# A hybrid decoder trunk: the strided pairs of the mixer wait for another mark, and the second sum of h is issued in more steps

## The chip, the cores and the metric

The kernel runs on one core of a Trainium2 chip. The time is that of one execution on the device in microseconds. Before the change it has a median of 2717.23 us over three runs (2716.2 to 2718.05). The profiled execution took 2714.47 us, with a span of 2712.6 us in its trace.

The engines are named as in the profile: PE is TensorE (matrix products), PEld its weight loads, DVE is VectorE, ACT is ScalarE, POOL is GpSimd, and SP is the queue that issues DMA transfers.

## The reference

Two layers (`DEPTH = 2`) work on 1024 tokens of width 1024, in float32:

```
for l in range(DEPTH):
    h = rmsnorm(x, norm1[l])
    proj = h @ w_in[l]                 # q, k, v of mixer A, q, k, v of mixer B, two gates
    o_a = dilated_mixture(qa, ka, va)  # 3 groups of 4 heads: (window, dilation) (128,1) (512,4) (2048,16)
    o_b = stick_breaking_attention(qb, kb, vb)           # 4 heads
    g_a, g_b = sigmoid(gate_pre + b_gate[l]) split in two
    x = x + (g_a * (o_a @ w_br[l, :OUT_A]) + g_b * (o_b @ w_br[l, OUT_A:])) @ w_o[l]
    h2 = rmsnorm(x, norm2[l])
    x = x + (gelu(causal_conv(h2 @ w_up[l], gate half)) * value half) @ w_down[l]
return rmsnorm(x, norm_f)
```

What matters here is the first half of a layer, the mixer: the product `h @ w_in[l]` and the attention of mixers A and B.

## The kernel before

**Products in two parts.** Each float32 operand is split into a high part and a rest (`split`, lines 129 and 130: a cast on ACT, a subtraction on DVE), and three matmuls make one product (high by high, high by rest, rest by high).

**Plain products and strided pairs.** In the mixer, `h` is held in two halves of the tokens, each in eight blocks of 128 features (`hh`, `hl` in the trace). Keys, queries and values of the first dilated group and of mixer B are plain products. All the other columns of `w_in` (group 1 and 2 of mixer A, which are read with a stride over the tokens, and the gates) are computed in pairs of column blocks by a scheme that makes seven products of half size do for eight. One of the seven is computed as a plain product (`ahead` in `pair`, `r_ps` in the trace, 14 units). The other six, in five accumulations, are the unit `run` in `pair_rest` (`i_a`, `i_c` in the trace): four pairs of keys and queries (`kqs`), two of values (`vs`) and eight of gates (`gates`). Each pair begins with seven opening stages: it loads its weights (`in_a`), POOL and the splits make combinations of their blocks, and the kept plain product is loaded into `u`.

**The sums of h.** The pairs also need sums of h's blocks, S[1] to S[4]. `block_sums` plans them as a list of small entries: S[3] after the marks B14 and B17, S[1] after N01s, S[2] after N11s, S[4] after the plain units. The same tile (`h_sum`) is worked on from one sum to the next: `first` makes S[1] on POOL, `further` turns it into the next sum with two DVE operations per block (lines 921 and 922), and `in_two` splits each block (`t_hi`, `t_lo`; S[4] is written into `hh`, `hl` of the first half). `series(after, t, f, lag, gap)` puts the sum of block i at step `i * gap` and its split `lag` steps later; each step is an entry of the list, an empty one too.

**What sets the order.** The order on PE is written out by hand: PE's instructions run as the program issues them. ACT, DVE, POOL and SP have a planner, which takes what is ready by priority. The priority follows the place in the program; the splits of attention's parts (`p0h`, `p0l`) and the folds are raised by 200 places.

`attend` goes through the attention items: B00 to B17 (mixer B), N00, N01, N10, N11 (the first dilated group, two pairs of heads), T00 to T17 (the other two groups). An item has scores, turns (transposes of a block of probabilities, line 701 for N) and applies (products with v, line 713 for N); a turn's result is split (`p0h` on ACT, `p0l` on DVE) before the apply reads it. The scores of the next item stand between the turns and applies of the one before where they can. `late`, the last apply of an item, is put behind the first turn of the next item. An item's mark with an "s" (N11s) is set when its last score has been issued.

After each score, turn and apply `attend` calls `dense.advance(rate)`. It first calls `aside`, which takes one entry from the list of sums if its marks are there, then adds the rate (0.85 for the N items) and, for each whole number, makes one `step` of the dense stream: two blocks of a product, six matmuls. A unit of the dense stream is chosen by `choose`: the first of `main` if its marks are there (a strided pair only when the plain list is empty), else a plain unit, else a gate pair, but those only after a first strided pair has started. The next unit is chosen and made ready ahead of its turn, one opening stage a step. If nothing can be chosen, `step` does nothing and `advance` sets the sum of rates to zero. When the first strided pair starts, all that is left of the list of sums is issued at once.

T00 can't begin before its keys are fetched, which is set by a count of dense steps after the pairs of both values and of the first keys and queries are done (`fetch`, `at`); until then `until` calls `aside` and `step` in turn, with no attention between.

Of the kernel before, what the change touches and what calls it, by code (L numbers as in the profile page):

```python
# [47 lines left out]
def f32(ap):  # L48
    return ap.bitcast(F32)
# [3 lines left out]
def trunk_kernel(ctx, tc, x, norm1, w_in, b_gate, w_br, w_o, norm2, w_up, conv_w, conv_b, w_down, norm_f, out, depth=None, probe=None):  # L53
# [71 lines left out]
    def quarter(name, dtype=F32, c=HF):  # L125
        return sb.tile([P, 2048 // c, c], dtype, tag="xa", bufs=4, name=name)

    def split(hi, lo, src):
        act.copy(hi, src)  # L129
        dve.tensor_tensor(lo, src, f32(hi), ALU.subtract)  # L130
# [315 lines left out]
    def new_s(t):  # L446
        hi, lo = big("t_hi", F32R), big("t_lo", F32R)
        S[t] = [tuple(x.rearrange("p a (b c) -> p (a b) c", c=HF)[:, i, :] for x in (hi, lo)) for i in range(4)]
# [428 lines left out]
    def half(n, k):  # L877
        return [(H[n][0][:, 4 * k + i, :], H[n][1][:, 4 * k + i, :]) for i in range(4)]
# [13 lines left out]
            if i == 1:  # L892
                yield

    def block_sums():


        keep = {}
        S.clear()

        def at(t, i):
            if t == 3 and i < 2:
                if "o" not in keep:
                    keep["o"] = sb.tile([P, 2, HF], F32, tag="ot", name="h_sum2")
                return keep["o"][:, i, :]
            if "r" not in keep:
                keep["r"] = quarter("h_sum")
            return keep["r"][:, i, :]

        def first(t, a, b, i):  # L910
            r, (ah, al), (bh, bl) = at(t, i), a()[i], b()[i]
            pool.tensor_tensor(r, f32(al), f32(bl), ALU.subtract)
            pool.tensor_tensor(r, r, f32(ah), ALU.add)
            pool.tensor_tensor(r, r, f32(bh), ALU.subtract)

        def further(t, a, i):
            if t == 4:

                S[4] = half(0, 0)
            r, (ah, al) = keep["r"][:, i, :], a()[i]  # L920
            dve.tensor_tensor(r, f32(ah), r, ALU.subtract)
            dve.tensor_tensor(r, r, f32(al), ALU.add)

        def in_two(t, i):
            if t not in S:
                new_s(t)
            split(*S[t][i], at(t, i))

        b11, b12, b21, b22 = (lambda n=n, k=k: half(n, k) for k in range(2) for n in (1, 0))
        todo = []  # L930

        def plan(after, steps):

            for k in range(max(steps) + 1):
                todo.append((after, lambda fs=steps.get(k, ()): [g() for g in fs]))

        def series(after, t, f, lag, gap):
            steps = {}
            for i in range(4):
                steps.setdefault(i * gap, []).append(lambda i=i: f(i))  # L940
                steps.setdefault(i * gap + lag, []).append(lambda i=i: in_two(t, i))
            plan(after, steps)

        def third(i):
            return lambda: first(3, b22, b12, i)

        def cast(i):
            return lambda: in_two(3, i)

        plan({"B14"}, {0: [third(0)], 6: [third(1)]})  # L950
        plan({"B17"}, {0: [third(2)], 1: [cast(0)], 4: [cast(1)], 6: [third(3)], 9: [cast(2)], 14: [cast(3)]})
        series({"N01s"}, 1, lambda i: first(1, b12, b11, i), 7, 6)
        series({"N11s"}, 2, lambda i: further(2, b22, i), 1, 1)
        series({"plain", "01", "v0"}, 4, lambda i: further(4, b21, i), 1, 1)
        return todo

# [106 lines left out]
    def pair_kq(dense, l, g, pr):  # L1063
        off = 256 * g + P * pr

        def put(c, n, x, psum):
            hi = small("kq_h", F32R)
            lo = small("kq_l", F32R) if psum else x.bitcast(F32R)
            hv, lv, xv = (t if t is x and psum else t.rearrange("p (r j) -> p r j", r=4) for t in (hi, lo, x))
            if c:  # L1070
                act.mul(hv, xv, -SCALE)
                dve.scalar_tensor_tensor(lv, xv, -SCALE, f32(hv), ALU.mult, ALU.subtract)
            else:
                act.copy(hv, xv)
                dve.tensor_tensor(lv, xv, f32(hv), ALU.subtract)
            for src, kind in ((hv, 2), (lv, 1)) if c else ((hv, 3), (lv, 4)):
                there = tk[pr][:, :, 6 * (g - 1) + kind, n * P : (n + 1) * P]
                nc.sync.dma_start(there.rearrange("r p j -> p r j"), f32(src))
            if (c, n) == (1, 1):
                dense.done.add(f"{g}{pr}")  # L1080

        return pair(dense, l, (OFF_KA + off, OFF_QA + off), True, put)

    def pair_v(dense, l, g):


        def turn(c, n, f):
            tp = bank("s", "v_t")
            for r in range(4):
                pe.transpose(tp[:, r * P : (r + 1) * P], f[:, r * P : (r + 1) * P], ident)  # L1090
            for r in (0, 2):
                tw = tp[:, r * P : (r + 2) * P].rearrange("p (r h c) -> p r h c", r=2, h=2)
                vv = small("vv", F32R).rearrange("p (r h c) -> p r h c", r=2, h=2)
                act.copy(vv[:, :, :, 0:64], tw)
                dve.tensor_tensor(vv[:, :, :, 64:128], tw, f32(vv[:, :, :, 0:64]), ALU.subtract)
                for h in range(2):
                    there = tv[c][h, r : r + 2, :, g - 1, n * P : (n + 1) * P]
                    nc.sync.dma_start(there.rearrange("r p c -> p r c"), f32(vv[:, :, h, :]))
            if (c, n) == (1, 1):
                dense.done.add(f"v{g}")  # L1100

        def put(c, n, x, psum):
            f = x
            if psum:
                f = small("vf")
                act.copy(f.rearrange("p (r j) -> p r j", r=4), x)
            dense.at(4, lambda: turn(c, n, f))

        off = OFF_VA + 256 * g
        return pair(dense, l, (off, off + P), True, put)  # L1110
# [35 lines left out]
    def mixer(l, pending):  # L1146
# [9 lines left out]
        dense = Dense()  # L1156
        vs = {g: pair_v(dense, l, g) for g in (1, 2)}
        kqs = {(g, pr): pair_kq(dense, l, g, pr) for pr in range(2) for g in (1, 2)}
# [2 lines left out]
        dense.seven = [rest() for _, rest, _ in gates]  # L1161
        order = [vs[1], *(kqs[g, 0] for g in (1, 2)), vs[2], *(kqs[g, 1] for g in (1, 2)), *gates]
        dense.loads = [load for _, _, load in order]
        dense.side = [({"B02"}, zeros)] * (l == 0) + block_sums()

        def kq(name, pr, after, off, scale):
            offk, offq = (OFF_KB, OFF_QB) if name == "b" else (OFF_KA, OFF_QA)
            return [
                (None, after, keys(("k" + name, pr), l, offk + off), False),
                (name + str(pr), after, queries(("q" + name, pr), l, offq + off, scale), False),  # L1170
            ]
# [3 lines left out]
            ("v0", set(), values("v0", l, OFF_VA), False),  # L1175
            *kq("0", 0, {"B07s"}, 0, -SCALE),
            *kq("0", 1, {"B17s"}, P, -SCALE),
            (None, {"N11s"}, vs[1][1](), True),
            *((None, {"N11s"}, kqs[g, 0][1](), True) for g in (1, 2)),
            (None, {"N11s"}, vs[2][1](), True),  # L1180
            *((None, {"N11s"}, kqs[g, 1][1](), True) for g in (1, 2)),
        ]
        items = []
        for pr in range(2):
# [30 lines left out]
        todo = [(n, e0 + i) for e0 in range(0, KD, 2) for n in range(2) for i in range(2)]  # L1215
# [632 lines left out]
    with tc.manual_schedule(engines={mybir.EngineType.PE}):  # L1848
        pending = first()
        next(pending)  # L1850
        for l in range(depth):
            pending = mixer(l, pending)
            pending = ffn(l, pending, enter(l + 1) if l + 1 < depth else leave)
# [21 lines left out]
```

## Time and profile before

| | |
|---|---|
| median of three runs | 2717.23 us |
| profiled execution | 2714.47 us |
| its span | 2712.6 us |
| PE busy | 2657.8 us |
| DVE busy | 2105.9 us |
| ACT busy | 1330.4 us |
| POOL busy | 742.1 us |

A row of the profile's timeline gives the start in the span, the duration, the engine, the line of the kernel, what is written from what, the shapes, and how many instructions it merges. In brackets stands the idle time of the engine before the row and what ended it. PE's matmuls overlap, so that the distance from one start to the next says what one takes. A row of the table of stretches gives its bounds, its length, the busy time of PE, PEld, DVE, ACT and POOL with their counts, the granted clock of PE as a share of full speed, the busy share of the DMA engines, and GB/s.

### The profile page before, as it was taken

To read this page: it belongs to the slowest core of one execution; us is meant where nothing else is said; L and a number is where in the kernel's file an instruction comes from. 1 tells how busy PE (TensorE), PEld (TensorE's weight loads), DVE (VectorE), ACT (ScalarE), POOL (GpSimd) and SP (SyncE) were. 2 spreads that over 40 slices of the span, in tenths; PEclk is the share of its full clock that TensorE was granted. 3 is DMA by queue.
4 is the path that set the end of the run, shared out by engine and by line. 5 is a ranking of instruction groups with operands and counts; after the bars stand their busy time and mean duration, and the time that the engine had idled before them with its cause. 6 is when DMAs were issued, how large, how long until landed. Compare 5 with 4: busy or idle time off the path is not lost. (4 is left out here: it accounts for less than half of the span.)

```text
span 2712.6 us, 37003 instructions
## 1 busy us (share of the span) xinstructions
PE 2657.8 (98%) x13098; PEld 2227.5 (82%) x13098; DVE 2105.9 (78%) x3104; ACT 1330.4 (49%) x2458; POOL 742.1 (27%) x537
## 2 busy tenths in 40 slices
PE   8999999999999999999999989999999999999999
PEld 8877788888888888888888778888788888888888
DVE  6877876675789988897658888766858888998865
ACT  5656534464455555432335665434545545554225
POOL 2004133322233434321220041332212433443210
PEclk9999999999999999999999999999999999999999
DMA  4023389863235444688401234997722444446863
GB/s 153 20 80 123 123 229 246 207 226 121 85 117 171 141 154 147 223 320 320 154 32 36 84 111 136 250 230 211 248 85 79 148 152 143 171 141 253 333 246 122
DMA packets 397637, 445.72 MB, mean 164 GB/s; under 512 B 21660, under 2 KB 318988, under 8 KB 395916
## 3 DMA queue, kind: packets, MB, share of 16 engines
q1 hardware_dynamic: 397452, 443.35, 51.4%
q8 instruction: 104, 1.70, 0.3%
q14 instruction: 81, 0.66, 0.1%
HBM read 300.61 MB, written 142.67 MB: 163 GB/s over the span
## 5 line engine op out<-in xcount | busy, mean ns | idle before, releaser
L130 DVE TENSOR_TENSOR w_lo<-up_a,w_hi 128x512 fp32r<-128x512 f32 x240 | 237.2, 995 | 20.5 <-ACT w_hi L129 20.5
L129 ACT CAST w_hi<-up_a 128x512 fp32r<-128x512 f32 x240 | 149.5, 623 | 184.1 <-PE u_a L890 45.6
L1631 DVE TENSOR_TENSOR x<-x,d_ps 128x512 f32<-128x512 f32 (+1 forms) x228 | 152.2, 672 | 76.9 <-PE d_ps L1625 76.0
L1362 POOL TENSOR_TENSOR cv<-cv 128x512 f32<-128x512 f32 x88 | 132.1, 1513 | 248.8 <-DVE cv L1357 138.9
L130 DVE TENSOR_TENSOR w_lo<-w_raw,w_hi 128x512 fp32r<-128x512 f32 x176 | 132.5, 756 | 67.8 <-ACT w_hi L129 67.3
L129 ACT CAST w_hi<-w_raw 128x512 fp32r<-128x512 f32 x176 | 109.2, 621 | 125.9 <-PE o_ps L156 68.6
L129 ACT CAST w_hi<-in_a 128x512 fp32r<-128x512 f32 x140 | 86.8, 620 | 147.6 <-PE i_a L890 83.2
L130 DVE TENSOR_TENSOR g<-cv,g 128x512 fp32r<-128x512 f32 x154 | 152.4, 991 | 5.2 <-ACT g L129 2.7
L1623 PE MATMUL d_ps<-gd_in,w_hi 128*128 128x512 f32 (+1 forms) x340 | 130.2, 383 | 1.3 <-ACT w_hi L129 1.1
L1625 PE MATMUL d_ps<-gd_in,w_lo 128*128 128x512 f32 (+1 forms) x340 | 129.8, 382 | 0.0
L1624 PE MATMUL d_ps<-gd_in,w_hi 128*128 128x512 f32 (+1 forms) x340 | 129.7, 382 | 0.0
L889 PE MATMUL u_a<-hh,w_hi 128*128 128x512 f32 x320 | 124.7, 390 | 0.5 <-DVE u L1513 0.5
L889 PE MATMUL u_a<-t_hi,w_hi 128*128 128x512 f32 x320 | 124.6, 389 | 0.0
L891 PE MATMUL u_a<-t_hi,w_lo 128*128 128x512 f32 x320 | 124.5, 389 | 0.0
L890 PE MATMUL u_a<-hl,w_hi 128*128 128x512 f32 x320 | 124.5, 389 | 0.0
L891 PE MATMUL u_a<-hh,w_lo 128*128 128x512 f32 x320 | 124.5, 389 | 0.0
L890 PE MATMUL u_a<-t_lo,w_hi 128*128 128x512 f32 x320 | 124.5, 389 | 0.0
L130 DVE TENSOR_TENSOR w_lo<-in_a,w_hi 128x512 fp32r<-128x512 f32 x140 | 116.0, 828 | 4.1 <-ACT w_hi L129 3.7
L1018 POOL TENSOR_TENSOR in_a<-in_a 128x512 f32<-128x512 f32 x28 | 38.0, 1357 | 278.9 <-DVE w_lo L130 278.9
L627 DVE TENSOR_TENSOR_SCAN stay<-stay,zero 128x128 f32<-128x128 f32 (+3 forms) x64 | 89.0, 1390 | 32.2 <-ACT stay L625 31.6
L1623 PE MATMUL d_ps<-gd_in,wd 128*128 128x512 f32 (+1 forms) x292 | 113.9, 390 | 0.0
L129 ACT CAST g<-cv 128x512 fp32r<-128x512 f32 x154 | 95.0, 617 | 38.2 <-POOL cv L1362 29.7
(390 smaller groups left out, 8747.7 us busy)
## 6 DMA issues: line engine op xcount, KB each, us to landing
gd<-g SPq DMA_DIRECT2D x154, 512.0 KB, 3.7
gd_in<-gd SPq DMA_DIRECT2D x154, 512.0 KB, 6.4
up_a<-in_w_up_dram SPq DMA_DIRECT2D x80, 512.0 KB, 5.8
in_a<-in_w_in_dram SPq DMA_DIRECT2D x56, 512.0 KB, 6.2
w_raw<-in_w_in_dram SPq DMA_DIRECT2D x104, 256.0 KB, 3.0
t_kq<-tk SPq DMA_DIRECT2D x64, 384.0 KB, 7.8
wd_raw<-in_w_down_dram SPq DMA_DIRECT2D x22, 1024.0 KB, 13.0
gin<-gs SPq DMA_DIRECT2D x32, 512.0 KB, 4.4
```

Source lines behind the costliest of these rows:

```text
L129: act.copy(hi, src)
L130: dve.tensor_tensor(lo, src, f32(hi), ALU.subtract)
L627: dve.tensor_tensor_scan(rev, rev, zero[:, 0:1].to_broadcast([P, L]), 1.0, ALU.mult, ALU.add)
L889: pe.matmul(o, w[0][:, c], rh, start=(first and i == 0), stop=False, skip_group_check=True)
L890: pe.matmul(o, w[0][:, c], rl, start=False, stop=False, skip_group_check=True)
L891: pe.matmul(o, w[1][:, c], rh, start=False, stop=(last and i == 3), skip_group_check=True)
L1018: pool.tensor_tensor(a11, a22, a11, ALU.subtract)
L1362: return lambda: pool.tensor_tensor(dst, a, b, ALU.subtract)
L1623: pe.matmul(o[:, sub], wh[:, c], gh[:, sub], start=(i == 0 and k in (0, 4, 5)), stop=False, skip_group_check=True)
L1624: pe.matmul(o[:, sub], wh[:, c], gl[:, sub], start=False, stop=False, skip_group_check=True)
L1625: pe.matmul(o[:, sub], wl[:, c], gh[:, sub], start=False, stop=(i == m - 1), skip_group_check=True)
L1631: dve.tensor_tensor(x, x, o[:, sub], ALU.add)
```

## The change

The second sum is planned with a gap of 2 steps in place of 1, so that each block's sum and each block's split have an entry of their own. Behind them stands a new entry, which waits for nothing and sets the mark T2. The six strided pairs of keys, queries and values in `main` wait for T2 and no longer for N11s. `block_sums` gets the set of marks for it. What is computed stays the same.

```
-    def block_sums():
+    def block_sums(done):
...
-        series({"N11s"}, 2, lambda i: further(2, b22, i), 1, 1)
+        series({"N11s"}, 2, lambda i: further(2, b22, i), 1, 2)
+        todo.append((set(), lambda: done.add("T2")))
         series({"plain", "01", "v0"}, 4, lambda i: further(4, b21, i), 1, 1)
...
-        dense.side = [({"B02"}, zeros)] * (l == 0) + block_sums()
+        dense.side = [({"B02"}, zeros)] * (l == 0) + block_sums(dense.done)
...
-            (None, {"N11s"}, vs[1][1](), True),
-            *((None, {"N11s"}, kqs[g, 0][1](), True) for g in (1, 2)),
-            (None, {"N11s"}, vs[2][1](), True),
-            *((None, {"N11s"}, kqs[g, 1][1](), True) for g in (1, 2)),
+            (None, {"T2"}, vs[1][1](), True),
+            *((None, {"T2"}, kqs[g, 0][1](), True) for g in (1, 2)),
+            (None, {"T2"}, vs[2][1](), True),
+            *((None, {"T2"}, kqs[g, 1][1](), True) for g in (1, 2)),
```

## The prediction

> **What bounds the kernel now.** First the page's busy times and its chain of waits, then the busy time by stages, then the order of TensorE's instructions, and last the rows of the engines that feed it.
>
> ```profile
> span 2712.6 us, 37003 instructions
> PE 2657.8 (98%) x13098; PEld 2227.5 (82%) x13098; DVE 2105.9 (78%) x3104; ACT 1330.4 (49%) x2458; POOL 742.1 (27%) x537
> ```
>
> TensorE (PE) is busy 98% of the span: whatever leaves it idle is paid in full, and there are 2712.6 - 2657.8 = 55 us of idle time that a better order could win. The change moves a unit of PE's work, so I look at the stages around it, in both layers:
>
> ```profile
> 314.00:326.00 12.00, 12.00 (x64) 10.05 (x64) 12.00 (x20) 7.79 (x18) 6.76 (x4) 1.00 0.52 154
> 326.00:339.00 13.00, 12.08 (x65) 9.90 (x64) 12.63 (x24) 6.62 (x13) 0.33 (x1) 1.00 0.20 69
> 339.00:395.00 56.00, 56.00 (x260) 46.32 (x259) 41.20 (x59) 20.85 (x40) 22.68 (x16) 1.00 0.77 211
> 1671.00:1684.00 13.00, 12.05 (x65) 9.89 (x64) 12.63 (x24) 6.59 (x14) 0.57 (x1) 1.00 0.24 78
> ```
>
> After the stretch's bounds and length stand the busy us of PE, its weight loads, VectorE (DVE), ScalarE (ACT) and GpSimd (POOL). From 339 to 395 us PE has no idle time at all. From 326 to 339 it is idle 0.92 us, and DVE is full: 12.63 of 13. Layer 1 repeats it at 1671. PE's rows there (start, duration; the idle time before it in brackets):
>
> ```profile
> 313.71 0.28 PE L585 MATMUL z<-kt,ql 128*128 128x256 f32 x1
> 313.83 0.40 PE L155 MATMUL r_ps<-hh,w_hi 128*128 128x512 f32 x1
> 315.22 0.60 PE L701 MATMUL t<-ident,p 128*128 128x128 f32 x4
> ...
> 326.03 0.28 PE L713 MATMUL o<-p0h,v 128*128 128x256 f32 x1
> 326.51 0.40 PE L889 MATMUL i_a<-t_hi,w_hi 128*128 128x512 f32 x1
> 327.90 0.49 PE L701 MATMUL t<-ident,p 128*128 128x128 f32 x3
> 328.14 0.47 PE L889 MATMUL i_a<-t_hi,w_hi 128*128 128x512 f32 x1
> 329.62 0.28 PE L713 MATMUL o<-p0h,v 128*128 128x256 f32 x1
> 330.05 0.50 PE L889 MATMUL i_c<-t_hi,w_hi 128*128 128x512 f32 x1
> 331.57 0.60 PE L701 MATMUL t<-ident,p 128*128 128x128 f32 x4
> 331.92 0.31 PE L713 MATMUL o<-p0h,v 128*128 128x128 f32 x1
> 332.92 0.33 PE L713 MATMUL o<-p0l,v 128*128 128x128 f32 x1 [0.69 <-DVE p0l L130]
> 333.37 0.40 PE L889 MATMUL i_c<-t_hi,w_hi 128*128 128x512 f32 x1
> 334.77 0.27 PE L701 MATMUL t<-ident,p 128*128 128x128 f32 x1
> 336.26 0.28 PE L713 MATMUL o<-p0h,v 128*128 128x256 f32 x1
> 338.61 0.22 PE L713 MATMUL o<-p0h,v 128*128 128x128 f32 x1
> 338.81 0.48 PE L889 MATMUL i_c<-hh,w_hi 128*128 128x512 f32 x1
> ```
>
> I call six 512-wide matmuls of the dense stream a chunk: 315.22 - 313.83 = 1.39 us. The last score of item N11 is issued at 313.71, and N11s is set. The item's turns (`t`, L701) and applies (`o`, L713) follow, with chunks between them as cover. The last plain product ends at 326.03, and the first strided pair takes over without a gap at 326.51. Between the apply at 326.03 and the chunk at 338.81 stand six chunks of the pair. With `a` for apply and `t` for turn: a0, c1, t2, c2, a1, c3, t3, a2, c4, t4, c5, a3, c6, a4, and c7 at 338.81.
>
> **The change, part by part.** No arithmetic is added or removed.
>
> *When the mark comes.* The side list gives up one entry at each advance, the call after each score, turn or apply. The plan for B17 has 15 entries (0 to 14) and the first sum's 26 (3 x 6 + 7 = 25, from 0). From B17's mark to N11s the items give 12 + 11 + 4 + 8 = 35 advances: the rest of N00 with three of N01's scores; N01 with N00's last apply and its own; N10's four scores; N10 up to N11's last score. So 41 - 35 = 6 entries of the first sum are left when N11s is set. After it come 16 advances: five in N10 (score, t3, a2, t4, a3) and eleven in N11. Before, the pair is free at once and starts at the ninth, when the plain units have run out, just after a0; this is what the rows show. After the change the second sum takes 8 entries (steps 0 to 7) in place of 5, and the mark one more: 6 + 8 + 1 = 15, so T2 is set at the fifteenth advance, just after a3.
>
> *What PE does meanwhile.* At the ninth advance the plain list is empty, the gates may not start before a strided pair has, and `step` finds nothing: the advances in between run no dense work. One chunk goes at the fifteenth, the next after a4. Five of six chunks leave the tail and are done behind a4, in the stretch where PE is full: 5 x 1.39 = 6.95 us there. Everything from then on keeps its order, since T00's fetch hangs on the count of chunks, not on time.
>
> *What that frees.* From 326.03 to 338.81 are 12.78 us. The six chunks between the rows above take 1.39 + 1.48 + 1.52 + 1.40 + 1.49 + 1.4 = 8.7 (the fifth from the end of t4 at 334.77, the sixth as the others), the attention's own issue some 2.65, and the rest, 1.4, is waiting. After: 2.65 + one chunk of 1.4 + the new waits W, then the five chunks, 6.95. So c7 comes at 326.03 + 4.05 + 6.95 + W = 337.03 + W in place of 338.81: the layer loses W - 1.8 us. Without waits it would win. W is what the trace doesn't show, so it is bounded by the rows that feed the applies:
>
> ```profile
> 325.35 1.79 DVE L130 TENSOR_TENSOR hl<-h_sum,hh 128x512 fp32r<-128x512 f32 x2
> 327.66 0.67 DVE L600 TENSOR_TENSOR on<-o,fold 64x512 f32<-64x512 f32 x1
> 328.86 0.54 DVE L130 TENSOR_TENSOR p0l<-t,p0h 128x384 fp32r<-128x384 f32 x1
> 329.33 0.67 DVE L988 TENSOR_TENSOR rf<-q1s,r_ps 128x512 f32<-128x512 f32 x1
> 332.33 0.54 DVE L130 TENSOR_TENSOR p0l<-t,p0h 128x384 fp32r<-128x384 f32 x1
> 336.02 0.68 DVE L130 TENSOR_TENSOR p0l<-t,p0h 128x512 fp32r<-128x512 f32 x1
> ...
> 327.12 0.48 ACT L129 CAST p0h<-t 128x384 fp32r<-128x384 f32 x1
> 330.63 0.62 ACT L129 CAST hh<-h_sum 128x512 fp32r<-128x512 f32 x1 [2.50 <-DVE h_sum L922]
> 331.15 0.47 ACT L129 CAST p0h<-t 128x384 fp32r<-128x384 f32 x1
> ```
>
> Low end: each apply waits only for its own chain, 0.48 + 0.54 (p0h, p0l) and some 0.1 for three hand-overs. With t3 in between, a2 can start 1.15 us after t2, and so on; then c2 starts near 331.3 and W is about 1.2: the layer wins 0.6 us. High end: DVE keeps its whole order, so that the third and fourth parts come at 336.02 and later as now; then a3 ends at about 337, c1 and a4 at 338.9, W is 8.9 and the layer loses 7.1.
>
> I take a value nearer the low end, by the order of the planner. Up to a0 nothing that PE does has moved, and so the planner's order on DVE stands until p0l of t1 at 328.86: a1 can't start before 329.40, though PE is ready at 326.8. That is 2.6 us. After it, the turns are closer together, so that the five DVE operations which now fill the 3 us between the p0l at 328.86 and that at 332.33 shrink to about one (0.67): a2 waits 0.3. For a3, ACT first folds a1's bank, and DVE has that fold (0.67) and one more operation ahead of p0l: 1.5. a4 has c1 in front of it. W = 2.6 + 0.3 + 1.5 = 4.4, and the layer loses 4.4 - 1.8 = 2.6 us; two layers 5.2.
>
> *The second sum, spread out.* Its eight DVE sums and the splits are the same instructions. In the trace the sums already run long before their place in the program (next fence, 276.06), because DVE takes what is ready; so I cost the spreading at nothing. What hides it is that the splits' first reader, c1, comes later than before. Without that floating the splits (4 x 0.64 us on DVE) would stand between the p0l of the tail, which is inside the high end.
>
> *The pair's opening.* With `choose` later, all seven opening stages of the first pair come in one go at the fifteenth advance and no longer spread over four chunks: two loads on SP's queue, POOL's three sums, two splits, the load of the kept product, a third split. Behind them on SP's queue nothing of N11 waits. POOL's sum shows that the load floats:
>
> ```profile
> 269.71 1.28 POOL L1011 TENSOR_TENSOR in_a<-in_a 128x512 f32<-128x512 f32 x1
> 276.06 0.68 DVE L921 TENSOR_TENSOR h_sum<-hh,h_sum 128x512 f32<-128x512 f32 x1
> 277.26 0.68 DVE L130 TENSOR_TENSOR p0l<-t,p0h 128x512 fp32r<-128x512 f32 x1
> 277.99 0.39 PE L713 MATMUL o<-p0l,v 128*128 128x256 f32 x1 [2.48 <-DVE p0l L130]
> in_a<-in_w_in_dram SPq DMA_DIRECT2D x56, 512.0 KB, 6.2
> ```
>
> It runs 57 us before c1. I cost the opening at nothing; if it stayed where it is written, c1 would wait for 6.2 us of load, two POOL sums of 1.28 and a split of some 1.3, about 10 us per layer.
>
> *The idle itself.* The longest new gap, 2.6 us, has a neighbour in this trace: the 2.48 us before 277.99, after which matmuls keep their spacing; the clock in the stages above is 1.00. So no price is put on the gap. [...]
>
> The sum stands against the profiled execution's 2714.47 us (span 2712.6): 2719.7. That run lies 0.1% under the median of 2717.23, to which I add the same 5.2: 2722.4 us, +0.19%. About 0.2%, or 5.4 us, is what a measurement of this kernel can tell from no change.
>
> **The rivals.**
> - *DVE's order stays* (slower). For it: DVE is full, and ACT at 330.63 stood 2.50 us behind a sum of the last series and held up the p0h at 331.15. Against it: parts are given priority. It loses 4 to 7.1 us per layer, 8 to 14 in all: 2725 to 2731. It decides if the p0l of t3 starts later than 5 us after that of t1.
> - *The applies run free* (no loss). W falls below 3.1: from -0.6 to +1.3 us per layer, 2716.0 to 2719.8. For it: the bare chain is 1.15 us. Against it: the p0l at 328.86.
> - *The earlier wait goes* (faster). If the later sums no longer go ahead of the p0l at 277.26, part of the 2.48 us is won, with the low end at most 2 x (0.6 + 2.48) = 6.2: 2711. Against it: the sum at 276.06 is only 0.68 of that wait, and ready work keeps its turn.
> - *Nothing moves.* Were T2 set by the ninth advance, PE's order would stay: 2717.2. The count of 15 against 9 speaks against it.
> - *The opening is late* (slower): +10 per layer on top, about 2742.
> - *The clock drops* (slower): if a gap costs two chunks at half speed, 2 x 1.39 per layer on top, 5.2 + 5.6 = 10.8: 2728.
>
> **How the numbers follow.** The forecast, 1.3 to 4 us per layer (2719.8 to 2725.2), gets 0.60, about half of it above 5.4 us. DVE's order 0.13, applies free 0.13, the earlier wait 0.06, nothing moves 0.03, the opening 0.02, the clock 0.03. Slower by over 0.2%: 0.29 + 0.13 + 0.02 + 0.03 = 0.47. Within: 0.31 + 0.13 + 0.03 = 0.47. Faster: 0.06. The range, 2715.5 to 2730, leaves out the earlier wait, the late opening and the end of DVE's order, some 0.12.
>
> **What would show it.** Right: after the last plain product there are seven steps of N11 (a0, t2, a1, t3, a2, t4, a3) with no `i_a` chunk in between, then one, then the rest in a row; PE idle some 4 us there, named p0l; the stretch of pure dense work 5 chunks longer; the same order afterwards. Wrong: a chunk between a0 and a3; PE idle under 3 or over 6 us in that stretch; an `i_a` that waits for a `w_lo` or a load; or times that differ elsewhere, most of all before 313 us or after T00, where I expect nothing.

## The result and the profile after

The changed kernel has a median of 2725.76 us over six runs (2724.95 to 2731.47), against 2716.72 us (2712.28 to 2718.9) for the kernel before on the same chip. The ratio is 1.0041, with a 95% interval from 1.0028 to 1.0054: the change makes the kernel slower by 0.3 to 0.5%, some 11 us by the means of the runs, which the ratio compares; the medians differ by 9.0. The profiled execution took 2730.9 us. The head of its page:

```profile
span 2729.0 us, 37013 instructions
PE 2664.8 (98%) x13098; PEld 2232.8 (82%) x13098; DVE 2105.6 (77%) x3104; ACT 1329.8 (49%) x2458; POOL 744.8 (27%) x537
```

PE's matmuls are as many as before, and the busy times of DVE, ACT and POOL are the same within 3 us. Span minus busy PE is now 2729.0 - 2664.8 = 64 us, where it was 55. The rest of the loss is inside PE's busy time, which grew by 7. The table of stretches of the changed kernel, with stretches of before and one at the same place of layer 1, shows where both come from:

```profile
326.00:339.00 13.00, 8.95 (x39) 7.28 (x38) 10.75 (x19) 5.30 (x11) 3.04 (x2) 0.74 0.05 20
339.00:395.00 56.00, 56.00 (x257) 46.32 (x256) 38.38 (x55) 19.30 (x35) 19.20 (x14) 1.00 0.70 194
1682.00:1694.00 12.00, 7.95 (x33) 6.42 (x33) 9.80 (x17) 5.23 (x10) 2.13 (x2) 0.72 0.06 24
```

From 326 to 339 PE is idle 4.05 us in place of 0.92, and the granted clock, 1.00 before, is 0.74. Layer 1 repeats it. The next stretch is full again. Up to this stretch, and from its end at c7 to 406 us of the kernel before, PE's order of work is the same in both kernels, in layer 1 likewise, so the start of a given matmul can be compared:

| start of | before | after | difference |
|---|---|---|---|
| N11's last score, layer 0 | 313.71 | 314.18 | +0.47 |
| c7, layer 0 | 338.81 | 345.28 | +6.47 |
| N11's last score, layer 1 | 1658.47 | 1669.27 | +10.80 |
| c7, layer 1 | 1683.57 | 1700.37 | +16.80 |
| end of the span | 2712.6 | 2729.0 | +16.4 |

From N11's last score to c7 passed 25.10 us in both layers before, and 31.10 in both layers after. I call this the tail's length; it takes 6.0 us more per layer, 12.0 in all, which the ratio's interval (7.6 to 14.7 us) holds. The other 4.3 us lie between the two tails. Most of them seem to belong to this one execution: the kernel with the spread sum alone (below), whose time does not differ from before, has drifted by 3.7 us at the same place. A small part may come from a second change of order. In the attention items T, from 406 to 539 us of the kernel before and again in layer 1, turns, applies and chunks stand in a changed order: before, a turn starts at 406.25 and the chunk after it at 406.49; after, that chunk starts at 412.60 and the turn at 414.00. From 406 to 668 us the changed kernel falls back by another 2.9 us. But `gap_only`, with the order of before, falls back by 1.6 there too, and two kernels below with the changed order, `early_open` and `no_fourth`, by 1.3 and 2.4. So what this second change costs can't be told from drift. PE's rows in the first tail:

```profile
326.50 0.28 PE L713 MATMUL o<-p0h,v 128*128 128x256 f32 x1
...
326.98 0.49 PE L701 MATMUL t<-ident,p 128*128 128x128 f32 x3
328.57 0.38 PE L713 MATMUL o<-p0h,v 128*128 128x256 f32 x1 [1.10 <-ACT p0h L129]
330.11 0.39 PE L713 MATMUL o<-p0l,v 128*128 128x256 f32 x1 [1.17 <-DVE p0l L130]
...
330.51 0.63 PE L701 MATMUL t<-ident,p 128*128 128x128 f32 x4
330.89 0.31 PE L713 MATMUL o<-p0h,v 128*128 128x128 f32 x1
332.38 0.48 PE L713 MATMUL o<-p0l,v 128*128 128x128 f32 x1 [1.18 <-DVE p0l L130]
...
333.19 0.41 PE L701 MATMUL t<-ident,p 128*128 128x128 f32 x1
333.25 0.56 PE L713 MATMUL o<-p0h,v 128*128 128x256 f32 x1
334.42 0.58 PE L713 MATMUL o<-p0l,v 128*128 128x256 f32 x1 [0.60 <-DVE p0l L130]
...
335.22 0.63 PE L889 MATMUL i_a<-t_hi,w_hi 128*128 128x512 f32 x1
...
337.78 0.31 PE L713 MATMUL o<-p0h,v 128*128 128x128 f32 x1
...
338.17 0.69 PE L889 MATMUL i_a<-t_hi,w_hi 128*128 128x512 f32 x1
```

The order is a0, t2, a1, t3, a2, t4, a3, c1, a4, and then five chunks in a row, as predicted. The four waits in brackets sum to 4.05 us. And c1 takes from 335.22 to 337.78, 2.56 us, where a chunk takes 1.39. Stretches of one microsecond show the clock in the column behind POOL's:

```profile
330.00:331.00 1.00, 0.89 (x8) 0.89 (x8) 1.00 (x3) 0.00 (x0) 0.00 (x0) 1.00 0.00 0
331.00:332.00 1.00, 0.20 (x3) 0.05 (x1) 1.00 (x3) 0.69 (x2) 0.00 (x0) 0.90 0.47 184
332.00:333.00 1.00, 0.62 (x3) 0.62 (x3) 0.97 (x3) 0.98 (x2) 0.00 (x0) 0.50 0.20 78
...
337.00:338.00 1.00, 1.00 (x5) 0.81 (x3) 0.00 (x0) 0.00 (x0) 0.00 (x0) 0.50 0.00 0
338.00:339.00 1.00, 1.00 (x6) 0.91 (x6) 0.04 (x1) 0.64 (x2) 0.00 (x0) 0.69 0.00 0
339.00:340.00 1.00, 1.00 (x6) 0.84 (x5) 0.64 (x1) 0.40 (x2) 0.00 (x0) 1.00 0.00 0
```

It is halved from 331.8 to 338.6. What the waits hang on stands on DVE's and ACT's queues, DVE first:

```profile
324.44 1.78 DVE L130 TENSOR_TENSOR hl<-h_sum,hh 128x512 fp32r<-128x512 f32 x1
326.14 1.78 DVE L921 TENSOR_TENSOR h_sum<-hh,h_sum 128x512 f32<-128x512 f32 x1
...
328.44 1.15 DVE L130 TENSOR_TENSOR w_lo<-in_a,w_hi 128x512 fp32r<-128x512 f32 x1
329.51 0.55 DVE L130 TENSOR_TENSOR p0l<-t,p0h 128x384 fp32r<-128x384 f32 x1
329.98 0.67 DVE L989 TENSOR_TENSOR rf<-q1s,r_ps 128x512 f32<-128x512 f32 x1
330.57 0.68 DVE L922 TENSOR_TENSOR h_sum<-h_sum,hl 128x512 f32<-128x512 f32 x1
331.18 0.68 DVE L921 TENSOR_TENSOR h_sum<-hh,h_sum 128x512 f32<-128x512 f32 x1
331.78 0.55 DVE L130 TENSOR_TENSOR p0l<-t,p0h 128x384 fp32r<-128x384 f32 x1
332.25 0.68 DVE L130 TENSOR_TENSOR hl<-h_sum,hh 128x512 fp32r<-128x512 f32 x1
...
333.67 0.89 DVE L130 TENSOR_TENSOR p0l<-t,p0h 128x512 fp32r<-128x512 f32 x2
```

ACT in the same stretch of the same kernel:

```profile
327.39 0.62 ACT L129 CAST w_hi<-in_a 128x512 fp32r<-128x512 f32 x1 [2.39 <-POOL in_a L1019]
328.04 0.48 ACT L129 CAST p0h<-t 128x384 fp32r<-128x384 f32 x1
...
331.29 0.62 ACT L129 CAST hh<-h_sum 128x512 fp32r<-128x512 f32 x1 [1.88 <-DVE h_sum L922]
331.93 0.58 ACT L599 COPY fold<-o 64x512 f32<-64x512 f32 x1
332.54 0.58 ACT L129 CAST p0h<-t 128x512 fp32r<-128x512 f32 x1
```

`h_sum`, `hh` and `hl` are here the last sum of h, S[4], which is written into the first half. Its reader is far away, but its work stands between the parts, and it passes from DVE (sum) to ACT (cast) and back (subtraction).

### The profile page after: what moved, and what is told of

Its sections match the earlier page's. It is cut to its first block, busy times and chain, and to the rows that moved or that the text cites. A ratio compares the mean times of both kernels' runs of the same rounds, so it can differ in the third digit from the quotient of the medians.

```text
span 2729.0 us, 37013 instructions
## 1 busy us (share of the span) xinstructions
PE 2664.8 (98%) x13098; PEld 2232.8 (82%) x13098; DVE 2105.6 (77%) x3104; ACT 1329.8 (49%) x2458; POOL 744.8 (27%) x537
## 5 line engine op out<-in xcount | busy, mean ns | idle before, releaser
L1624 PE MATMUL d_ps<-gd_in,wd 128*128 128x512 f32 (+1 forms) x292 | 113.9, 390 | 0.0
L1626 PE MATMUL d_ps<-gd_in,wd 128*128 128x512 f32 (+1 forms) x292 | 112.8, 386 | 0.0
```

The costliest lines, as they stand in the source:

```text
L1624: pe.matmul(o[:, sub], wh[:, c], gh[:, sub], start=(i == 0 and k in (0, 4, 5)), stop=False, skip_group_check=True)
L1626: pe.matmul(o[:, sub], wl[:, c], gh[:, sub], start=False, stop=(i == m - 1), skip_group_check=True)
```

## The experiments

Theory A: the tail loses because five chunks that stood before the waits have left it, and the parts p0h and p0l come late since other ready work, above all S[4], stands ahead of them on ACT and DVE. Theory B: the halved clock is the main loss. Theory C: the spreading of the second sum, or the later opening of the first pair, costs the time. All ratios below are to the kernel before, run on the same chip in turn; the tail's length is that of layer 0 and layer 1.

| kernel | ratio, 95% interval | tail, us |
|---|---|---|
| before | 1 | 25.10, 25.10 |
| after | 1.0041 (1.0028 to 1.0054) | 31.10, 31.10 |
| gap_only | 1.0001 (0.9993 to 1.0010) | 25.07, 25.11 |
| mark_13 | 1.0058 (1.0045 to 1.0071) | 31.70, 31.78 |
| mark_17 | 1.0045 (1.0031 to 1.0059) | 31.19, 31.29 |
| fill | 1.0061 (1.0048 to 1.0073) | 31.78, 31.97 |
| fill_more | 1.0039 (1.0024 to 1.0054) | 30.39, 30.39 |
| early_open | 1.0038 (1.0023 to 1.0053) | 31.07, 31.23 |
| no_fourth | 0.9993 (0.9983 to 1.0002) | 24.96, 24.87 |
| second_pool | 1.0023 (1.0012 to 1.0033) | 25.94, 25.90 |
| after_fourth_pool | 1.0073 (1.0059 to 1.0087) | 36.17, 36.10 |
| before_fourth_pool | 1.0055 (1.0041 to 1.0069) | 35.52, 34.08 |
| after_cast_pool | 1.0057 (1.0042 to 1.0072) | 34.29, 34.22 |
| before_cast_pool | 1.0003 (0.9994 to 1.0011) | 26.84, 26.82 |

**gap_only: the spread sum alone, in the kernel before.**

```
-        series({"N11s"}, 2, lambda i: further(2, b22, i), 1, 1)
+        series({"N11s"}, 2, lambda i: further(2, b22, i), 1, 2)
```

> The kernel before with the second sum's gap of 2 alone; the pairs still wait for N11s and there is no mark T2. Theory A (the loss is PE's lost cover in N11's tail, with the clock's drop that follows from it): no chunk moves, so the time is that of before, 2716.7 us within 0.1%, and no window at half clock. Rival B (the planner's new order of the sums on DVE and ACT costs the time): about half of the change's loss or more, 2721 to 2726 us.

Its tail is that of before, and so is its time. The row of the stretch has the busy times of before (12.08, 9.90, 12.63 there):

```profile
326.00:339.00 13.00, 12.05 (x64) 9.86 (x63) 12.81 (x23) 6.60 (x14) 0.35 (x1) 1.00 0.18 62
```

The spreading alone costs nothing; the first half of theory C falls. The loss comes only with the mark.

**mark_13: the changed kernel with the sum's gap back at 1.** The mark comes three entries earlier, the first pair starts two advances earlier, behind a2 and no longer behind a3, and three chunks leave the tail in place of five.

```
-        series({"N11s"}, 2, lambda i: further(2, b22, i), 1, 2)
+        series({"N11s"}, 2, lambda i: further(2, b22, i), 1, 1)
```

> The changed kernel with the second sum's gap put back to 1, so that T2 is set at the advance 6 + 5 + 1 = 12 and the first pair starts at the 13th: three of the six chunks leave the tail and not five. Theory A: one wait of some 2.5 us before a1 and little behind it; the clock stays at 1.00, since a chunk follows a2; loss some 1.5 us per layer, 2720 us in all (ratio 1.001). If the loss were simply in proportion to the chunks moved: 3/5 of the change's 9 to 11 us, about 2722.5 us.

A miss: fewer chunks moved, and the tail is no shorter. One row of ACT and one of PE, both in the tail of layer 0:

```profile
328.07 0.62 ACT L129 CAST w_hi<-in_a 128x512 fp32r<-128x512 f32 x1 [5.66 <-POOL in_a L1019]
```

```profile
330.86 0.38 PE L713 MATMUL o<-p0h,v 128*128 128x256 f32 x1 [3.59 <-ACT p0h L129]
```

ACT stood 5.66 us before a split of the pair's weights that waits for POOL, with the part for a1 behind it. Here the opening of the pair, and not the fourth sum, makes the longest wait. So the loss does not go by the number of chunks that leave, but by when the parts come; the cover only decides whether that is felt.

**mark_17: two empty entries ahead of the mark**, which sends the sixth chunk behind a4 as well.

```
         series({"N11s"}, 2, lambda i: further(2, b22, i), 1, 2)
+        todo += [(set(), lambda: None)] * 2
         todo.append((set(), lambda: done.add("T2")))
```

> The changed kernel with two empty entries ahead of the mark: T2 comes at the 17th advance, after a4, and all six chunks leave the tail. Theory A: a4 gets a wait of its own of about 1 us and the whole first chunks run at half clock: 1 to 3 us more per layer than the change, 2728 to 2731 us (ratio 1.005). If the loss were in proportion to the chunks moved: 6/5 of the change's, 2728 us; the trace decides by the clock and the waits.

Another miss: 1 to 3 us more per layer were expected, and the tail is as long as after the change, within 0.2 us. No wait was left for the sixth chunk to cover: a3's part is the last that comes late.

**fill and fill_more: useless matmuls of 512 columns behind t2, t3 and t4**, where the change leaves PE idle: 9, 4 and 2 in the first kernel, 9, 4 and 9 in the second. They take no part's place; they only keep PE busy.

```
+            if self.main and not (self.plain or self.now or self.nxt or self.started):
+                self.idle += 1
+                for _ in range({2: 9, 4: 4, 6: 9}.get(self.idle, 0)):
...
+                    pe.matmul(self.warm, H[1][0][:, 0, 0:P], H[1][0][:, 0, :], start=True, stop=True, skip_group_check=True)
```

> The changed kernel with 15 matmuls of no use in each layer's tail (9 behind t2, 4 behind t3, 2 behind t4; they write a bank that nobody reads, the output stays the reference's). They add about 15 x 0.23 = 3.5 us of PE work per layer, into waits of some 4 to 5 us. Theory A, with the clock's drop as its second half: PE's clock stays at 1.00 in the tail, the chunk behind a3 takes 1.4 us in place of 2.56, and although work is added the time falls to about 2722 to 2723 us (ratio 1.002). If the clock has no part in it: as the changed kernel or slower, 2726 to 2730 us.

> The useless matmuls again, now 9, 4 and 9 behind t2, t3 and t4: in the run with 9, 4 and 2 the clock held to 335 us and then halved, behind the wait of 1.81 us for the p0l of t3 (the stretches 336 to 338 show 0.50), so the last wait is filled too. If the drop of the clock is a cost of its own: PE stays at 1.00 in both tails, the chunk behind a3 takes 1.4 us and not 2.6, and c7 comes about 1.5 us earlier than in that run (344.5 us in place of 345.98), some 2729 us in all. If the clock's drop only fills time that DVE and ACT need anyway: c7 at 346 or later.

The first is a miss: PE still waited 1.81 us for the last part, and the clock fell late. It is 0.87 over the stretch, and the tail is no shorter. In the second the clock holds, in both tails:

```profile
326.00:339.00 13.00, 11.94 (x64) 9.68 (x63) 11.19 (x19) 5.27 (x11) 3.43 (x3) 1.00 0.08 29
1682.00:1694.00 12.00, 10.96 (x56) 8.71 (x56) 10.06 (x19) 5.69 (x12) 1.56 (x1) 1.00 0.06 23
```

At full clock the tail is still 5.3 us longer than before. The parts of a1 and a2 come no earlier for it: a1's last wait ends 330.50 - 314.56 = 15.94 us after N11's last score, where it ended 330.11 - 314.18 = 15.93 after it in the changed kernel, and a2's 18.20 after it in both. The last wait, a3's, ends later, 21.44 us after the score in place of 20.24, so the filling has put it off by 1.2 us. From there to c7 pass 344.95 - 336.00 = 8.95 us in place of 345.28 - 334.42 = 10.86. So the halved clock costs 1.9 us, of which 31.10 - 30.39 = 0.7 are left as a gain here. It is the smaller part, and theory B falls as the main cause.

**early_open: the first pair's opening stages from where the kernel before issues them**, one per advance, with the chunks where the change has put them.

```
+            if "N11s" in self.done and self.main and not (self.plain or self.nxt or self.started):
+                name, _, gen, seven = self.main[0]
+                if seven:
+                    self.early = self.early or [name, gen, seven, 0]
+                    self.ready(self.early)
```

> The changed kernel, but the first pair's opening stages are issued one at an advance from the point where the kernel before issues them; its products still wait for T2. If the late opening is part of the loss (ACT stands 2.39 us before a w_hi that waits for POOL's sum of a11, with p0h of t1 behind it): that wait goes, a1 starts about 1 us earlier, each tail loses some 5 us and not 6, about 2723.5 us. If the opening is free, as the prediction had it: 6 us per layer as the changed kernel.

ACT's 2.39 us before POOL's sum are gone, and the p0h of t1 starts at 327.31 in place of 328.04. But DVE gets to the p0l only at 329.05, and the tail is what it was. The second half of theory C falls too.

**no_fourth: the changed kernel without the fourth sum.** Its eight sums and four splits per layer are left out, and the first half itself stands in their place.

```
-        series({"plain", "01", "v0"}, 4, lambda i: further(4, b21, i), 1, 1)
+        S[4] = half(0, 0)
```

> The changed kernel without the fourth sum: its eight sums and four splits per layer are left out (S[4] is then the unchanged first blocks of h, so the output isn't the reference's). DVE has 8.2 us less to do in each tail. If the waits of the applies are DVE's queue: W falls from about 5 to 2 to 3 us, with it the clock's drop shrinks or goes, a tail loses 0 to 2 us, 2717 to 2721 us in all. If the applies wait for their own chain alone: W stays and the time is that of the changed kernel, 2725 us.

Here is the cause. The row of the stretch, then DVE's parts, then PE's two waits that are left:

```profile
326.00:339.00 13.00, 12.12 (x66) 10.24 (x66) 7.20 (x13) 4.98 (x10) 1.67 (x2) 1.00 0.32 95
```

```profile
325.80 0.54 DVE L130 TENSOR_TENSOR p0l<-t,p0h 128x384 fp32r<-128x384 f32 x1
...
327.46 0.54 DVE L130 TENSOR_TENSOR p0l<-t,p0h 128x384 fp32r<-128x384 f32 x1
328.03 0.68 DVE L600 TENSOR_TENSOR on<-o,fold 64x512 f32<-64x512 f32 x1
328.75 0.89 DVE L130 TENSOR_TENSOR p0l<-t,p0h 128x512 fp32r<-128x512 f32 x2
```

```profile
328.06 0.33 PE L713 MATMUL o<-p0l,v 128*128 128x128 f32 x1 [0.34 <-DVE p0l L130]
...
329.50 0.39 PE L713 MATMUL o<-p0l,v 128*128 128x256 f32 x1 [0.54 <-DVE p0l L130]
```

All five chunks have left the tail as in the changed kernel, PE waits 0.9 us in place of 4.05, the clock stays at 1.00, and the tail is 0.1 to 0.2 us shorter than before the change. So lost cover alone costs next to nothing; it costs where work that can wait is queued ahead of the parts. (The kernel before without the fourth sum wasn't run. Its tail has 0.9 us of waits to lose, so the cover may be worth up to some 0.8 us without the sum too.) The fourth sum's absence also brings the pair's opening forward: ACT's split of the weights starts at 323.45 in place of 327.39. But in early_open ACT no longer waits for the opening at all, and that wins nothing. Whether the order of the sum's work counts, and not only how much of DVE's time it takes, is what the next kernels were for.

**after_fourth_pool and before_fourth_pool: the fourth sum's two operations per block on POOL**, in the kernel after and before.

```
+            eng = pool if t == 4 else dve
+            eng.tensor_tensor(r, f32(ah), r, ALU.subtract)
+            eng.tensor_tensor(r, r, f32(al), ALU.add)
```

> The changed kernel with the fourth sum's eight operations per layer on POOL and not on DVE; the result is unchanged. If the tail's waits are DVE's queue (without the fourth sum at all the tail lost nothing and the clock held): DVE has 5.4 us less in the tail, W falls by 2 to 4 us, the clock drops late or not at all, a tail loses 1 to 4 us and not 6, 2719 to 2724 us. Against it: POOL's use of the same memory can slow DVE's subtractions (one fourth sum took 1.78 us beside POOL and 0.68 without), and ACT's casts into hh wait for POOL: then 2725 us or more.

> The kernel before with the fourth sum's eight operations per layer on POOL. Its tail has 0.9 us of named waits per layer, so at most 2 us are to be won: 2715 to 2717 us if POOL is free enough. If POOL, which also makes the pairs' openings from 318 us on, becomes late with them: an i_a or i_c that waits for a w_lo or for hl, 2718 to 2725 us.

Both are slower than the kernels that they change, though DVE has less to do in the stretch (9.60 and 7.69 us of 13). A row of ACT in the first, and two in the second:

```profile
328.74 0.62 ACT L129 CAST hh<-h_sum 128x512 fp32r<-128x512 f32 x1 [4.42 <-POOL h_sum L923]
```

```profile
329.70 0.62 ACT L129 CAST hh<-h_sum 128x512 fp32r<-128x512 f32 x1 [5.45 <-POOL h_sum L923]
333.81 0.62 ACT L129 CAST hh<-h_sum 128x512 fp32r<-128x512 f32 x1 [3.49 <-POOL h_sum L923]
```

In both kernels the p0h for a0 comes next on ACT behind these casts: at 329.26 in the first, for a turn that PE issued at 318.71, and at 334.33 in the second, for one of 321.31. PE waits 4.7 us in one piece for this p0h, and 7.2 in the other kernel. Both waits stand before a0, ahead of all chunks that the change moves, so that the six chunks which the second kernel still has in its tail can't cover them. So a less busy DVE did not help here, while the chain passed through ACT ahead of the parts.

**after_cast_pool and before_cast_pool: the fourth sum's casts on POOL**, so that ACT has nothing of it.

```
+            if t == 4:
+                hi, lo = S[t][i]
+                pool.tensor_copy(hi, at(t, i))
+                dve.tensor_tensor(lo, at(t, i), f32(hi), ALU.subtract)
+                return
```

> The changed kernel, but the fourth sum's casts into hh are made by POOL and not by ACT; its sums and subtractions stay on DVE and the result is the same. If the parts wait because these casts stand ahead of p0h in ACT's queue, in order, and wait there for DVE's sums (1.88 us in the changed kernel, 4.4 and 5.4 us where the sums ran on POOL): the p0h come as soon as their turns are done, W falls by 1 to 3 us, a tail loses 2 to 5 us and not 6, 2719 to 2724 us. If it is DVE's full queue alone: the p0l stay where they are, 2725 us.

> The kernel before with the same edit. If ACT's queue is behind the 0.69 and 0.22 us waits of its tail: they go, at most 1 to 2 us over two layers, 2715 to 2717 us. If POOL becomes late with the pairs' openings: an i_a or i_c that waits, 2718 to 2724 us.

The stand moved to the other queue. DVE in the changed kernel's variant:

```profile
328.94 1.06 DVE L930 TENSOR_TENSOR hl<-h_sum,hh 128x512 fp32r<-128x512 f32 x1 [5.00 <-POOL hh L929]
...
332.32 0.54 DVE L130 TENSOR_TENSOR p0l<-t,p0h 128x384 fp32r<-128x384 f32 x1
```

DVE stood 5.00 us before a subtraction that nobody needs soon, and PE waited 3.1 us for the p0l behind it; the clock is 0.77 over the stretch. In the kernel before, the same edit costs 1.7 us per tail, the clock stays at 1.00, and the total does not differ clearly from before (at most 0.11% more, or 3.0 us, where the two tails together lose 3.5; what makes up for the rest was not followed). There the six chunks cover most of it. This pair compares the same queue with and without the cover: 34.29 - 26.84 = 7.5 us, the halved clock included.

**second_pool: the second sum's operations on POOL, in the kernel before**, which was to free DVE ahead of the 2.48 us wait at 277.99 and perhaps to beat both kernels (the edit is that of the fourth sum, with `t == 2`).

> The kernel before with the second sum's eight operations per layer on POOL and not on DVE. If the 2.48 us wait for the p0l before 277.99 comes from DVE being full of sums: 0.6 to 1.2 us per layer less in front of N11, 2715 us. If the wait comes from the splits of the first sum ahead of it, or POOL's use slows DVE: no gain, 2717 us or a little more. No change of PE's order and no drop of the clock in the tail are expected by either.

It is slower by 0.23%. The waits of PE around that place (engine, line, what is waited for, total, times, longest):

```profile
PE o L713 <- DVE p0l L130: 5.5, 2, 5.1
```

The longest wait grew from 2.48 to 5.1 us. The first four of POOL's sums took 1.59 to 1.73 us each where DVE's took 0.68, and DVE is as full as before: from 272 to 282 us it is busy 9.96 of 10 in both kernels, with 11 operations here, beside a POOL that is busy 9.84, and with 14 before, where POOL has 2.30.

## Why the prediction was right, and what it had too small

The forecast was 2722.4 us, +0.19%; measured is +0.41%, inside the range and on the side of slower. The mechanism is the predicted one: cover leaves the tail, and PE waits for parts that stand late in the queues. The size is about double, 6.0 us per layer against 2.6. The median of 2725.76 us lies just above the forecast's own interval (2719.8 to 2725.2) and in that of the rival "DVE's order stays" (2725 to 2731). That the range held it is owed in part to its width, since two terms were too small at once.

- *When the mark comes*, and *what PE does meanwhile*: right in the tail. The order has one chunk between a3 and a4 and five behind a4. "Everything from then on keeps its order" was wrong: from T00 on turns, applies and chunks shift against each other. The count of chunks to T00's fetch is as it was. The probable reason for the shift, not tested, is that `advance` sets its sum of rates to zero when `step` finds nothing.
- *The second sum, spread out*, at nothing: right (gap_only). *The opening*, at nothing: right for this order, since early_open has the same tail. In mark_13, where the pair starts two advances earlier, it made the 3.59 us wait.
- *W, the new waits*, 4.4 us: too small. From a0 to c7 are now 345.28 - 326.50 = 18.78 us. Take from it the attention's issue, 2.65, c1 at 1.39 and the five chunks, 6.95: 7.79 are left for waits and clock. The clock's share is read from the rows at half speed against the same rows of no_fourth: c1 2.56 against 1.40; a3 from its second part to c1 0.80 against 0.45; a4 0.39 against 0.20; the next chunk 1.67 against 1.46. That is 1.9, as much as fill_more gives (a2's slower rows lie ahead of a3's wait, and are taken as hidden by it). So W is 5.9, and the layer loses 5.9 - 1.8 = 4.1 by waits.
- Which wait: W is counted from start to start, and so are its parts here, each less the turn's and apply's own issue. From t2 to t3 pass 330.51 - 326.98 = 3.53 us with 0.67 of issue, so a1 waits 2.9 (forecast 2.6). From t3 to t4 pass 2.68 with some 0.8, so a2 waits 1.9 (forecast 0.3). From t4 to c1 pass 2.03 with 0.5 of issue and 0.35 of clock, so a3 waits 1.2 (forecast 1.5). Nearly the whole error is a2's. I had given it 0.3 us on the ground that the five DVE operations between the first two p0l would shrink to one; three stood there (`rf` and two steps of the fourth sum, 329.98 to 331.78). This is the step that failed: I had taken the priority of the parts to reorder DVE, and the fourth sum was still ahead of them. On ACT too a cast of the fourth sum (331.29, after 1.88 us of standing for it) came ahead of the fold and the p0h at 332.54.
- *DVE's order stays*, the rival, was forecast at 4 to 7.1 us per layer, to be decided by whether the p0l of t3 starts more than 5 us behind that of t1. It starts 333.67 - 329.51 = 4.16 us behind, against 7.16 before the change and 2.95 in no_fourth. So its price fits and its sign does not: the truth lies between it and the forecast, and part of the order stayed.
- *The idle itself*, costed at nothing: wrong. The rival "the clock drops" had 2.8 us per layer, from an estimate of two chunks at half speed; it is 1.9. By the 2.48 us before 277.99 in the kernel before I had held shorter gaps to be safe. They are not: the longest idle time in the tail was 1.18 us, and the clock fell to 0.50. Shorter waits of the kernel before itself show it too (last section).
- *What would show it* named PE idle times over 6 us or under 3 as wrong: they are 4.05. That this fits is luck in part, since they belong to a W of 5.9 and not of 4.4; the rest of W stands in rows that the profile counts as busy. The idle times were to be named p0l; three are, and the first, 1.10, is named p0h, which stood on ACT behind the weights' split of the opening. "The same order afterwards" is not met. Times elsewhere, where I expected nothing, differ by up to 4.3 us between the tails, little more than gap_only's drift.

What stays open: whether the changed mark would be free with the fourth sum kept but queued behind N11's parts. That order wasn't tried. no_fourth, which doesn't have the work at all, is the best that it could come to: a tail 0.1 to 0.2 us shorter than before, and a total of 0.9983 to 1.0002. No kernel here beats the one before.

## What to carry to other kernels

Work that PE can do at any time is worth most just ahead of the operands that come late; before moving it, list what stands ahead of those operands on each engine's queue, with the chain between queues, and assume that it stays there. A chain such as sum, cast, subtraction over two engines can leave each queue standing until the other engine's step is done, 1.88 us here on ACT, which is busy for 49% of the span; moving one link to POOL moved the stand and lengthened it to 3.5 to 5.5 us. And look at the granted clock after every wait of PE, and not only at the longest gap: here three idle times of 1.10 to 1.18 us close together were followed by half clock, and one of 2.48 us was not.

## What the runs showed of the hardware that was not expected

- The clock fell to 0.50 in the changed kernel after idle times of 1.10, 1.17 and 1.18 us with small matmuls between (331.8 to 338.6), and not in the kernel before after one of 2.48 us (277.99), where it stays at 1.00 from 270 to 290 us. The kernel before has such drops as well, after waits that are shorter than 2.48 us: 2.17 us before 184.48 and before 1528.89, 1.89 before 1416.48, and 1.47 before 1770.62. The columns are those of the table of stretches:

```profile
185.00:187.00 2.00, 2.00 (x7) 1.61 (x6) 1.96 (x5) 0.92 (x3) 0.00 (x0) 0.50 0.32 88
270.00:290.00 20.00, 16.09 (x86) 12.93 (x84) 19.09 (x30) 11.57 (x23) 4.22 (x3) 1.00 0.30 93
1417.00:1419.00 2.00, 2.00 (x6) 1.58 (x6) 1.49 (x3) 1.86 (x5) 0.00 (x0) 0.50 0.00 0
1530.00:1531.00 1.00, 1.00 (x4) 0.81 (x3) 0.95 (x3) 0.60 (x2) 0.00 (x0) 0.50 0.25 71
1772.00:1774.00 2.00, 2.00 (x7) 1.61 (x6) 1.52 (x5) 1.34 (x5) 0.00 (x0) 0.50 1.04 261
```

  So in these rows the length of a wait does not tell whether the clock falls; what does is not shown here. The longer single waits were followed by a lower clock: 3.59 us in mark_13 (0.74 from 326 to 339 us), 4.73 in after_fourth_pool (0.64 there), 7.15 in before_fourth_pool (0.71 there) and 5.09 in second_pool (0.50 from 280 to 282).
- A DVE sum or subtraction on 128x512 took 0.68 us (331.18 and 332.25 in the changed kernel), and 1.78 beside POOL's sums (326.14 and 324.44, with POOL at work from 324.04 to 329.04). The rows give the times and not the cause. In after_fourth_pool, whose sums were put on POOL to relieve DVE, three `hl` on DVE from 322.44 on took 5.14 us, with POOL at work from 322.05 to 328.70.
